# Where two feed-forwards split their matmul operands: VectorE in place of GpSimd, and activations split per column in the second

## The chip, the cores and the metric

The kernel runs on one core of a Trainium2 chip. The metric is the device time of the whole kernel in microseconds (us): the median of three runs. Its engines are TensorE (PE in the profile), which multiplies matrices and accumulates in PSUM; VectorE (DVE), ScalarE (ACT) and GpSimd (POOL), which work element by element in SBUF; and SyncE (SP), which here only starts transfers. Each engine works through its own queue in order. PEld is TensorE's loading of the stationary operand.

## What is computed

Two blocks of two layers each, on 256 rows of 1024 numbers (float32). The first block's layers have mixers (recurrent, dilated and latent attention) and a feed-forward, which is what changes; the second block's layers have attention and a table of 16384 experts per layer ("peer"), 128 of which are gathered for each row.

```python
# first block, layer l
h = rms_norm(x, attn_norm_g[l])
...
x = x + concatenate([ya, yb, yc]) @ w_out[l]
h = rms_norm(x, ffn_norm_g[l])
x = x + (silu(h @ ffn_w_gate[l]) * (h @ ffn_w_up[l])) @ ffn_w_down[l]
# second block: rows of its context and of x
s1, s2 = q1 @ sub_keys[0].T, q2 @ sub_keys[1].T     # two top-16, their 256 sums, top-16 of these
u = u_tab[expert]
act = gelu(einsum('nhkd,nd->nhk', u, hb))
out = einsum('nhk,nhkd->nd', softmax(top_s) * act, v_tab[expert])
```

The width of the feed-forward is 2816, that is 22 columns of 128.

## The kernel before, in words

**Splits.** Each float32 matmul is made of three: both operands are split into a high part (rounded, dtype F32R) and a low part (the rest), and hi*hi, hi*lo and lo*hi are accumulated (`mm3`, L183 to 191). `Net.split` (L172 to 181) makes the high part with a copy on ScalarE (L177) and the low part with a subtraction (L181) on VectorE, or on GpSimd where its argument `eng2` says so. Weights come as 512 KB tiles (128 x 1024); `Weights.load` splits them and goes through the letters of `low` in turn, "gv" being GpSimd, VectorE and so on.

**A feed-forward** (`First.ffn`, L509 to 547) has two loops of 22 steps. The gate/up loop loads two weight tiles (wgu) per column c, multiplies both with the normed and transposed x (hT) into one PSUM tile pgu, and makes the activation: a tanh on ScalarE (L523), then on VectorE a multiplication and addition in SBUF (L524), a product with the gate half (L525) and one with the up half (L526). The result of all columns, ffact, stands in SBUF in float32. The down loop loads one tile of ffn_w_down (wd) per step k, splits it, splits column k of ffact into a pair ffak (ffak_hi on ScalarE, ffak_lo on GpSimd), and adds 12 matmuls to four PSUM tiles pd. Behind the loop x_state (L547, four instructions on VectorE) adds pd to x.

**The two feed-forwards** are f0 (layer 0, L1791) and f1 (layer 1, L1820). f0 has two weight buffers of each kind and the letters "gv": of 44 wgu_lo 22 are on GpSimd, of 22 wd_lo 11. f1 has six buffers and "v": its 44 wgu_lo are on VectorE, but 5 of its 22 wd_lo (those that go through wd2) and all 22 ffak_lo are on GpSimd. Between them lies the mixer of layer 1, m1, whose norm makes nr_y on GpSimd, nr_t on VectorE, and transposes x into hT.

**What runs beside them.** The second block's context rows are routed and gathered at the same time. The routing (`route_block`, L1296 to 1392) is a chain of top-k steps on VectorE for each of two blocks of 128 rows; its ends are ef (L1386), the slots slot_e (L1389) and slot_eT (L1392, after a transpose stp on TensorE). The gather (`peer_gather`) asks for rows by an indirect DMA that GpSimd starts (ug, L1425), and makes a product of each with hm: on GpSimd (L1415, with ScalarE's sum L1416) for the first 60, on VectorE (a custom instruction, L1418) after these. After f1 come the final norm of the first block and the norm of the second (hxn, hxs, hxv, then nr_y and ns_y), and the weights wqkv of the first attention.

**The order** is not written out by hand: a scheduler with a model of the engines' time puts the instructions of all these parts into one order per engine, by rank and by when it thinks that they can start. A change of one part therefore moves rows of the others too.

## Time and profile before

| | |
|---|---|
| median of three runs | 3541.01 us (3537.23, 3541.01, 3547.21) |
| the profiled execution | 3555.65 us, its span 3553.9 us |
| mean granted TensorE clock | .935 of full |
| PE busy | 88% of the span |
| DVE busy | 74% |
| POOL busy | 54% |
| ACT busy | 40% |

The profile is one execution, 14.6 us longer than the median; times within it are microseconds from the start of its span. f0 takes the stretch from some 240 (gate/up) and 530 (down) to 627.5, m1 the one to 925, f1 the one from 925 (gate/up) and 1052.6 (down) to 1128.2. A share of busy time over the whole span says little about one of these stages, so the rows below are cut by stage. "PEclk" is the granted clock as a share of the full one.

### The profile page before, as it was taken

The page shows a single profiled execution, that of the slowest core. Times are in us where ns is not written, and L with a number is a line of the kernel's source. Part 1 is how long each engine was busy: PE and PEld are TensorE (multiplying, and loading weights), DVE is VectorE, ACT ScalarE, POOL GpSimd, SP SyncE. Part 2 cuts the span into 40 slices and gives each one's busy share as a digit, 9 for nine tenths or more (in the row PEclk, how much of TensorE's full clock was granted, in tenths as well). Part 3 has the DMA queues.
Part 4 walks back from the last instruction along what each step waited for, and adds up shares of the span by engine and source line. Part 5 has one row for each costly group of instructions (what it writes and reads, how often), then busy time and mean ns, then how long its engine had stood idle before and what let it go on. Part 6 is the DMA issues. An engine that isn't in the chain of part 4 may idle for free. (4 is left out here: it accounts for less than half of the span.)

```text
span 3553.9 us, 58408 instructions
## 1 busy us (share of the span) xinstructions
PE 3114.9 (88%) x22044; PEld 2575.2 (72%) x22044; DVE 2635.4 (74%) x5055; ACT 1426.0 (40%) x2195; POOL 1920.3 (54%) x1368
## 2 busy tenths in 40 slices
PE   8979997688896768879878899999888899999999
PEld 6758895566795558867557658756668899986887
DVE  5647789774897789999875784675677826789777
ACT  4234543443543454433323333323454343443454
POOL 2113228656667576667557657666211465544665
PEclk9999999899898879989989999999899999999999
DMA  6555554667897567778768779878423454544555
GB/s 205 174 165 162 161 161 155 205 218 238 301 331 248 174 224 243 240 276 312 247 232 306 274 265 322 306 280 322 143 68 118 154 178 155 167 155 137 183 191 172
DMA packets 260970, 761.46 MB, mean 214 GB/s; under 512 B 26064, under 2 KB 81424, under 8 KB 260688
## 3 DMA queue, kind: packets, MB, share of 16 engines
q1 hardware_dynamic: 127856, 410.50, 34.5%
q0 software_dynamic: 79456, 289.18, 23.7%
q10 hardware_dynamic: 53376, 58.05, 5.0%
q8 instruction: 173, 2.83, 0.3%
q14 instruction: 109, 0.89, 0.1%
HBM read 753.44 MB, written 4.19 MB: 213 GB/s over the span
## 5 line engine op out<-in xcount | busy, mean ns | idle before, releaser
L1582 PE MATMUL aT<-h_hi,u_lo 128*128 128x256 f32 x2048 | 595.6, 292 | 53.6 <-POOL u_lo L1567 26.7
L1580 PE MATMUL aT<-h_hi,u_hi 128*128 128x256 f32 x2048 | 595.0, 291 | 7.5 <-ACT u_hi L1564 6.8
L1581 PE MATMUL aT<-h_lo,u_hi 128*128 128x256 f32 x2048 | 588.4, 288 | 0.0
L1650 POOL TENSOR_TENSOR v_lo<-v_raw,v_hi 128x512 fp32r<-128x512 f32 x256 | 398.7, 1564 | 247.3 <-ACT v_hi L1649 223.4
L1567 POOL TENSOR_TENSOR u_lo<-u_raw,u_hi 128x512 fp32r<-128x512 f32 (+1 forms) x256 | 362.7, 1425 | 293.0 <-ACT u_hi L1564 284.8
L1425 POOL DMA_INDIRECT ug<-in_peer_u,slot_e x256 | 311.8, 1218 | 285.5 <-DVE act L1418 122.2
L1649 ACT ACTIVATE v_hi<-v_raw 128x1024 fp32r<-128x1024 f32 x256 | 270.8, 1059 | 477.6 <-issue 222.0
L1564 ACT ACTIVATE u_hi<-u_raw 128x1024 fp32r<-128x1024 f32 x256 | 269.5, 1058 | 477.4 <-PE aT L1581 216.2
L1582 PEld LDWEIGHTS aT<-h_hi,u_lo 128*128 128x128 f32 x2048 | 400.8, 196 | 68.3 <-DVE u_lo L1567 30.5
L1580 PEld LDWEIGHTS aT<-h_hi,u_hi 128*128 128x128 f32 x2048 | 402.6, 197 | 14.7 <-ACT u_hi L1564 9.0
L1581 PEld LDWEIGHTS aT<-h_lo,u_hi 128*128 128x128 f32 x2048 | 402.4, 196 | 4.2 <-issue 4.2
L1664 PE MATMUL acc<-v_hi,w_lo 128*128 128x512 f32 x1024 | 339.2, 413 | 60.2 <-DVE w_lo L181 59.5
L1567 DVE TENSOR_TENSOR u_lo<-u_raw,u_hi 128x512 fp32r<-128x512 f32 (+1 forms) x256 | 262.5, 1027 | 163.1 <-ACT u_hi L1564 138.7
L1449 POOL DMA_INDIRECT vg<-in_peer_v,slot_eT x256 | 262.6, 1026 | 142.1 <-PE pv L1454 59.7
L1664 PE MATMUL acc<-v_lo,w_hi 128*128 128x512 f32 x1024 | 331.4, 405 | 0.1
L1664 PE MATMUL acc<-v_hi,w_hi 128*128 128x512 f32 x1024 | 308.6, 411 | 5.2 <-ACT w_hi L177 5.2
L1415 POOL TENSOR_TENSOR ug<-ug,hm 128x1024 f32<-128x1024 f32 x106 | 263.4, 2489 | 65.9 <-DMA ug<-in_peer_u,slot_e 62.3
L1651 DVE TENSOR_TENSOR v_lo<-v_raw,v_hi 128x512 fp32r<-128x512 f32 x256 | 203.5, 795 | 116.0 <-ACT v_hi L1649 102.9
L1664 PEld LDWEIGHTS acc<-v_hi,w_lo 128*128 128x128 f32 x1024 | 192.4, 195 | 119.6 <-DVE w_lo L181 74.7
L181 DVE TENSOR_TENSOR w_lo<-d_A,w_hi 128x256 fp32r<-128x256 f32 x256 | 264.0, 1033 | 3.7 <-ACT w_hi L177 3.5
L1418 DVE CUSTOM_DVE_ANT_0 ug<-ug,hm 128x1024 f32<-128x1024 f32 x150 | 212.3, 1423 | 37.9 <-DMA ug<-in_peer_u,slot_e 35.4
L1664 PEld LDWEIGHTS acc<-v_lo,w_hi 128*128 128x128 f32 x1024 | 199.2, 196 | 45.9 <-issue 2.0
(659 smaller groups left out, 7539.3 us busy)
## 6 DMA issues: line engine op xcount, KB each, us to landing
u_raw<-in_u_columns SPq DMA_DIRECT2D x256, 512.0 KB
v_raw<-in_peer_v SPq DMA_DIRECT2D x256, 512.0 KB
adaw<-in_ada_w ACTq DMA_DIRECT2D x96, 512.0 KB
wgu<-in_ffn_w_gate SPq DMA_DIRECT2D x44, 512.0 KB
wgu<-in_ffn_w_up SPq DMA_DIRECT2D x44, 512.0 KB
wd<-in_ffn_w_down SPq DMA_DIRECT2D x44, 512.0 KB
wpq<-in_peer_w_q SPq DMA_DIRECT2D x32, 512.0 KB
wqkv<-in_w_qkv SPq DMA_DIRECT2D x24, 512.0 KB
```

The costliest lines, as they stand in the source:

```text
L181: e.tensor_tensor(lo, src, hi.bitcast(F32), op=ALU.subtract)
L1415: nc.gpsimd.tensor_tensor(u, u, hm, op=ALU.mult)
L1425: nc.gpsimd.indirect_dma_start(out=u, out_offset=None, in_=ut, in_offset=bass.IndirectOffsetOnAxis(ap=slots[b][0][:, j : j + 1], axis=0))
L1449: loads.append(nc.gpsimd.indirect_dma_start(out=four[q], out_offset=None, in_=vt, in_offset=bass.IndirectOffsetOnAxis(ap=slots[b][1][:, to ...
L1564: nc.scalar.activation(uh, u, AF.Copy)
L1567: e.tensor_tensor(ul[:, o:m], u[:, o:m], uh[:, o:m].bitcast(F32), op=ALU.subtract)
L1580: nc.tensor.matmul(o, uh[:, k], self.hh[:, k], start=k == 0, stop=False)
L1581: nc.tensor.matmul(o, uh[:, k], self.hl[:, k], start=False, stop=False)
L1582: nc.tensor.matmul(o, ul[:, k], self.hh[:, k], start=False, stop=k == KD - 1)
L1649: nc.scalar.activation(vh, v, AF.Copy)
L1650: nc.gpsimd.tensor_tensor(vl[:, 0:512], v[:, 0:512], vh[:, 0:512].bitcast(F32), op=ALU.subtract)
L1664: nc.tensor.matmul(self.acc[2 * b + hf], x[:, bs], y[:, hf * 512 : (hf + 1) * 512], start=s0, stop=s1)
```

## The change

In f0 the letter of the scope is "v", so all 44 wgu_lo and 22 wd_lo are on VectorE, and so are the 22 ffak_lo, since `split` is called without `eng2`. In f1 the 5 wd_lo of wd2 move to VectorE, and `early=True` replaces ffact by a pair of tiles, ffact_hi in zone "x" and ffact_lo in a new zone "y" (22528 bytes of each partition): the last product of a column goes back into ffth, and the column is split at once, high part on ScalarE and low part on VectorE. The down loop of f1 takes its operand from this pair and splits no activation. In all 82 subtractions go from GpSimd to VectorE. Line numbers of the new kernel are up to 11 higher from here on (x_state L558, slot_e L1400, the gather's products L1426 and L1429, its DMA L1436).

```diff
@@ -506,13 +506,17 @@
                 xs = x[:, b, hf * 512 : (hf + 1) * 512]
                 nc.vector.tensor_tensor(xs, pss[hf][b], xs, op=ALU.add)
 
-    def ffn(self, l, x, after=None, more=None):
+    def ffn(self, l, x, after=None, more=None, early=False):
+
 
         nc, n, a = self.nc, self.n, self.a
         hT, _ = self.norm_T(x, self.vcol("ffn_norm_g", l, 8), "hT2")
         if after:
             after()
-        act = self.zones["x"].tile([P, KF, S], F32, name="ffact")
+        if early:
+            act = self.zones["x"].tile([P, KF, S], F32R, name="ffact_hi"), self.zones["y"].tile([P, KF, S], F32R, name="ffact_lo")
+        else:
+            act = self.zones["x"].tile([P, KF, S], F32, name="ffact")
         for c in range(KF):
             ps = self.psum("pgu")
             for i, name in enumerate(("ffn_w_gate", "ffn_w_up")):
@@ -523,7 +527,11 @@
             nc.scalar.activation(th, ps[:, :S], AF.Tanh, scale=0.5)
             nc.vector.tensor_scalar(th, th, 0.5, 0.5, op0=ALU.mult, op1=ALU.add)
             nc.vector.tensor_tensor(th, ps[:, :S], th, op=ALU.mult)
-            nc.vector.tensor_tensor(act[:, c], ps[:, S:], th, op=ALU.mult)
+            if early:
+                nc.vector.tensor_tensor(th, ps[:, S:], th, op=ALU.mult)
+                n.split(th, *part(act, c))
+            else:
+                nc.vector.tensor_tensor(act[:, c], ps[:, S:], th, op=ALU.mult)
         wd = a["ffn_w_down"][l].rearrange("(k p) c -> p k c", p=P)
         pss = [self.psum(f"pd{i}") for i in range(4)]
         for k in range(KF):
@@ -535,9 +543,12 @@
                     two = self.zones["x"].pair([P, 2, D], "wd2")
                 w = part(two, k % 2)
                 raw = ws.plain(wd[:, k : k + 1], 1, D, "wd")
-                n.split(raw[:, 0], *w, eng2="gv"[k % 2])
-            ak = self.z.pair([P, S], "ffak")
-            n.split(act[:, k], *ak, eng2="g")
+                n.split(raw[:, 0], *w, eng2="v")
+            if early:
+                ak = part(act, k)
+            else:
+                ak = self.z.pair([P, S], "ffak")
+                n.split(act[:, k], *ak)
             for b in range(2):
                 for hf in range(2):
                     n.mm3(pss[2 * b + hf], part(ak, slice(b * P, (b + 1) * P)), part(w, slice(hf * 512, (hf + 1) * 512)), k == 0, k == KF - 1)
@@ -1705,7 +1716,6 @@
 GATHERS = 58
 MORE = 56
 UFIRST = EARLY + GATHERS + MORE - P
-LOW = "gv"
 POOL_DOTS = 3
 GATHER_CLASSES = ((32, 8), (512, 5), (1024, 2), (4096, 1))
 ATTN_CLASSES = (
@@ -1788,8 +1798,8 @@
                 for _ in itertools.islice(gather, SOON):
                     pass
                 slots.append(next(routed))
-            with f.scope("f0", FFN_ZONES, 2, {"w": 4}):
-                f.ffn(0, x, more=Weights(n, cw, 2, nc.sync, 2, LOW))
+            with f.scope("f0", FFN_ZONES, 2, {"w": 4}, "v"):
+                f.ffn(0, x, more=Weights(n, cw, 2, nc.sync, 2))
         tside.close()
         gside = cside.enter_context(ExitStack())
         gp[:] = [pool(gside, "g_g0", 2, side="right")]
@@ -1817,8 +1827,8 @@
                     pass
                 at[0] = tc.cur_priority
 
-        with f.scope("f1", FFN_ZONES, 6, {"w": 6}, "v", 4):
-            f.ffn(1, x, lambda: gather_on(GATHERS))
+        with f.scope("f1", dict(FFN_ZONES, y=((22528, 1),)), 6, {"w": 6}, "v", 4):
+            f.ffn(1, x, lambda: gather_on(GATHERS), early=True)
         fx.close()
         for l in range(L):
             last = l == L - 1
```

The scheduler's order changes with it. Three places:

VectorE at the end of f0, before: the second block's routing (csc to slot_e) and the four x_state.

```order
L1356 TENSOR_TENSOR csc_2305<-csc_2305 128x512 x2
L1356 TENSOR_TENSOR csc_2305<-csc_2305 128x256 x2
L1356 TENSOR_TENSOR i1o<-csc_2305 128x128
L1356 TENSOR_TENSOR i2o<-csc_2305 128x128
L1386 SCALAR_TENSOR_TENSOR ef<-i1o,i2o 128x128
L1389 CAST slot_e_3995<-ef 128x128
L547 TENSOR_TENSOR x_state<-pd_5684,x_state 128x512
L547 TENSOR_TENSOR x_state<-pd_5685,x_state 128x512
L547 TENSOR_TENSOR x_state<-pd_5686,x_state 128x512
L547 TENSOR_TENSOR x_state<-pd_5687,x_state 128x512
```

The last rows of the routing, down to the slots of the second block, stand ahead of x_state.

VectorE at the end of f0, in the changed kernel: csc_2305, v, i are the second block's routing at its first and second top-k step.

```order
L1324 MAX v_3997<-csc_2305 128x8 x3
L1403 CAST slot_eT_3777<-stp 128x128
L1324 MAX v_3997<-csc_2305 128x8 x9
L1323 MATCH_REPLACE csc_2305<-v_3997,csc_2305 128x128
L1325 MAX_INDEX i_3998<-v_3997,csc_2305 128x8 x3
L558 TENSOR_TENSOR x_state<-pd_5684,x_state 128x512
L558 TENSOR_TENSOR x_state<-pd_5685,x_state 128x512
L558 TENSOR_TENSOR x_state<-pd_5686,x_state 128x512
L558 TENSOR_TENSOR x_state<-pd_5687,x_state 128x512
L1325 MAX_INDEX i_3998<-v_3997,csc_2305 128x8 x9
L1324 MAX v_3997<-csc_2305 128x8
```

The rest of this routing, down to the slots, now stands behind x_state, between the rows of m1.

GpSimd at the start of m1, before: ug are products and requests of the gather, nr_y the norm of m1, w_lo one of its weights.

```order
L1415 TENSOR_TENSOR ug<-ug,hm_3945 128x1024 x2
L1425 DMA ug<-in_peer_u,slot_e_3776 128x1024 x2
L1415 TENSOR_TENSOR ug<-ug,hm_3945 128x1024
L212 TENSOR_TENSOR nr_y<-nv,mhalf 128x2
L1415 TENSOR_TENSOR ug<-ug,hm_3945 128x1024
L1425 DMA ug<-in_peer_u,slot_e_3776 128x1024
L181 TENSOR_TENSOR w_lo<-w,w_hi 128x896
```

Nearly all products of f0's time stand ahead of these rows.

GpSimd at the start of m1, in the changed kernel: these are also the first requests and products of the gather.

```order
L1420 DMA hm_3945<-d_crows 128x1024
L1436 DMA ug<-in_peer_u,slot_e_3776 128x1024 x2
L1426 TENSOR_TENSOR ug<-ug,hm_3945 128x1024 x2
L1436 DMA ug<-in_peer_u,slot_e_3776 128x1024 x2
L1426 TENSOR_TENSOR ug<-ug,hm_3945 128x1024
L181 TENSOR_TENSOR w_lo<-w,w_hi 128x896
L212 TENSOR_TENSOR nr_y<-nv,mhalf 128x2
L1426 TENSOR_TENSOR ug<-ug,hm_3945 128x1024
```

No split of f0 is left on GpSimd, and nr_y stands behind the first three products of all and a w_lo; in the kernel before seven products stood ahead of it, from f0 on.

VectorE at the end of f1, before: ISA ug,act are the gather's products (each followed by its read of the sum, act), hxs the sums of the norm.

```order
L547 TENSOR_TENSOR x_state<-pd_10249,x_state 128x512
L547 TENSOR_TENSOR x_state<-pd_10250,x_state 128x512
L547 TENSOR_TENSOR x_state<-pd_10251,x_state 128x512
L1418 ISA ug,act_3944<-ug,hm 128x1024
L1418 ISA act_3944 128x1
L1116 ISA hxj,hxs<-hxn,final_g 128x512
L1116 ISA hxs 128x1
L547 TENSOR_TENSOR x_state<-pd_10252,x_state 128x512
L1116 ISA hxj,hxs<-hxn,final_g 128x512
```

One product stands between the third x_state and the fourth.

VectorE at the end of f1, in the changed kernel: ident is a copy for the attention that follows.

```order
L558 TENSOR_TENSOR x_state<-pd_10297,x_state 128x512
L1429 ISA ug,act_3944<-ug,hm 128x1024
L1429 ISA act_3944 128x1
L558 TENSOR_TENSOR x_state<-pd_10298,x_state 128x512
L558 TENSOR_TENSOR x_state<-pd_10299,x_state 128x512
L1429 ISA ug,act_3944<-ug,hm 128x1024
L1429 ISA act_3944 128x1
L1038 CAST ident_10741<-c_all 128x128
L558 TENSOR_TENSOR x_state<-pd_10300,x_state 128x512
L1429 ISA ug,act_3944<-ug,hm 128x1024
L1429 ISA act_3944 128x1
L1127 ISA hxj,hxs<-hxn,final_g 128x512
```

From the first x_state to hxv five products stand in the changed kernel and two in the one before. In both six stand directly ahead of the first x_state.

## Rows read from the trace of the kernel before

**Rows 1.** The page: busy time of each engine, share of the span, instructions

```profile
PE 3114.9 (88%) x22044; PEld 2575.2 (72%) x22044; DVE 2635.4 (74%) x5055; ACT 1426.0 (40%) x2195; POOL 1920.3 (54%) x1368
```

**Rows 2.** Busy time of each engine by stretch, granted clock, DMA share

```profile
core 0: us, PE busy (x) PEld busy (x) DVE busy (x) ACT busy (x) POOL busy (x), PEclk, DMA share, GB/s
240.00:530.00 290.00, 274.71 (x1956) 256.00 (x1956) 215.89 (x442) 146.11 (x244) 86.64 (x66) 0.99 0.49 155
530.00:617.10 87.10, 70.17 (x265) 54.28 (x265) 86.83 (x288) 29.51 (x51) 72.42 (x44) 0.88 0.49 159
617.10:627.50 10.40, 0.47 (x1) 0.18 (x1) 10.33 (x18) 3.45 (x6) 6.95 (x4) 0.76 0.45 164
627.50:925.00 297.50, 236.30 (x1647) 173.01 (x1647) 187.69 (x321) 124.20 (x238) 189.93 (x111) 0.86 0.69 228
925.00:1052.60 127.60, 127.60 (x1058) 127.30 (x1056) 123.09 (x160) 63.79 (x94) 77.84 (x48) 1.00 0.90 321
1052.60:1128.20 75.60, 66.65 (x265) 52.59 (x264) 61.93 (x61) 27.87 (x43) 68.29 (x46) 0.91 0.72 246
1128.20:1152.00 23.80, 0.10 (x1) 0.00 (x0) 16.07 (x38) 6.66 (x12) 8.40 (x7) 0.56 0.88 318
```

**Rows 3.** Waits, 530 to 627.5: engine, line, for what; us, times, longest

```profile
PE pd L191 <- POOL ffak_lo L181: 9.1, 3, 6.4
...
PE stp L1391 <- DVE ef L1386: 7.8, 1, 7.8
...
PE pd L190 <- POOL wd_lo L181: 4.1, 2, 2.3
```

**Rows 4.** VectorE in order of time, 604 to 628: start, length, line, tiles

```profile
604.53 2.42 DVE L1341 TENSOR_SCALAR pm<-pm 128x128 int32<-128x128 int32 x1
...
625.00 2.48 DVE L547 TENSOR_TENSOR x_state<-pd,x_state 128x512 f32<-128x512 f32 x4
```

**Rows 5.** ffth in f0: min/median/max ns, first and last start

```profile
L524 DVE TENSOR_SCALAR ffth<-ffth x21: 280/2319/2549, 278.3 to 526.0; 128x256 f32<-128x256 f32 x21
L525 DVE TENSOR_TENSOR ffth<-pgu,ffth x21: 398/425/426, 280.7 to 526.6; 128x256 f32<-128x256 f32 x21
```

**Rows 6.** wgu_lo in f0, by engine

```profile
L181 DVE TENSOR_TENSOR wgu_lo<-wgu,wgu_hi x22: 1205/1225/1227, 256.0 to 520.6; 128x1024 fp32r<-128x1024 f32 x22
L181 POOL TENSOR_TENSOR wgu_lo<-wgu,wgu_hi x22: 2362/2399/3619, 259.5 to 522.6; 128x1024 fp32r<-128x1024 f32 x22
```

**Rows 7.** GpSimd in order of time, start of m1

```profile
628.66 2.35 POOL L1415 TENSOR_TENSOR ug<-ug,hm 128x1024 f32<-128x1024 f32 x1 [4.16 <-DMA ug<-in_peer_u,slot_e]
631.11 0.73 POOL L212 TENSOR_TENSOR nr_y<-nv,mhalf 128x2 f32<-128x2 f32 x1
```

**Rows 8.** TensorE in order of time, start of m1, idle before it in brackets

```profile
638.37 1.94 PE L415 MATMUL fps<-c_all,x_state 128*128 128x128 f32 x8 [8.87 <-DVE hT_lo L420]
```

**Rows 9.** VectorE by group, 925 to 1052.6: busy us, mean ns

```profile
L181 DVE TENSOR_TENSOR wgu_lo<-wgu,wgu_hi 128x1024 fp32r<-128x1024 f32 x40 | 69.2, 1735 | 3.6 <-ACT wgu_hi L177 3.6
L1418 DVE CUSTOM_DVE_ANT_0 ug<-ug,hm 128x1024 f32<-128x1024 f32 x24 | 31.3, 1308 | 0.0
```

**Rows 10.** Waits, 1052.6 to 1152: engine, line, for what; us, times, longest

```profile
PE pd L190 <- POOL wd_lo L181: 4.5, 2, 3.1
...
PE pd L189 <- ACT ffak_hi L177: 2.6, 1, 2.6
...
PE pd L191 <- POOL ffak_lo L181: 1.9, 2, 1.4
```

**Rows 11.** VectorE in order of time, end of f1 and the norm

```profile
1114.83 3.38 DVE L1418 CUSTOM_DVE_ANT_0 ug<-ug,hm 128x1024 f32<-128x1024 f32 x1
...
1130.89 1.22 DVE L1418 CUSTOM_DVE_ANT_0 ug<-ug,hm 128x1024 f32<-128x1024 f32 x1 [2.96 <-DMA ug<-in_peer_u,slot_e]
...
1132.04 1.88 DVE L547 TENSOR_TENSOR x_state<-pd,x_state 128x512 f32<-128x512 f32 x3
...
1140.50 1.23 DVE L1418 CUSTOM_DVE_ANT_0 ug<-ug,hm 128x1024 f32<-128x1024 f32 x1 [1.93 <-DMA ug<-in_peer_u,slot_e]
```

## What the change should do to the time

> **What bounds the kernel now.** I read the page's engine line first [rows 1]: TensorE is busy for 3114.9 of 3553.9 us and VectorE for 2635.4, so neither bounds the whole span, and the change is worth what its own stages can give back. So the second view is the table of stretches, cut where the stages of the two feed-forwards begin and end [rows 2]. The reader is to see four things in it. In the first feed-forward's gate/up stretch (240 to 530) TensorE has 274.7 of 290 us: it is the bound there, nearly. In the down projection after it (530 to 617.1) VectorE is busy for 86.83 of 87.1 us: VectorE is the bound, TensorE works 70.2 us at a mean granted clock of .88 (that is 61.7 us at the full 2.4 GHz), and TensorE then stands for 10 us more until 627.5. In the second feed-forward's gate/up stretch (925 to 1052.6) TensorE never stops. In its down projection (1052.6 to 1128.2) TensorE works 66.65 of 75.6 us at .91 (60.7 at full clock), and VectorE has slack.
>
> Then the waits of the first down projection [rows 3]: TensorE waits 9.1 us for GpSimd's ffak_lo, 4.1 for GpSimd's wd_lo, and at the end 7.8 for VectorE's ef, which belongs to the routing of the second block of rows. The list of VectorE's work in order of time shows why [rows 4]: the last matmul of pd ends at 617.1, but the four x_state additions start only at 625.00, because the routing stands ahead of them in VectorE's queue; its last part alone runs from 604.53 to 625.00.
>
> Last, what makes VectorE so full. The multiplication of ffth (L524, 128x256) takes 280 ns at best and 2319 at the median of 21 in the first feed-forward, while the next one on the same engine (L525), which reads PSUM, never leaves 398 to 426 [rows 5]. GpSimd's wgu_lo takes 2.36 to 2.40 us [rows 6]: the multiplication sits out one of these nearly every time.
>
> **The Trainium skill on this.** The page "SBUF — State Buffer", section "Who interferes with whom", says that VectorE and GpSimd share one pair of ports as an exclusive lock, taken by a VectorE instruction in a two-port mode or with two SBUF inputs, and that one with at most one SBUF input outside these modes doesn't contend. The rows on L524 and L525 agree. The same rule of the Trainium skill speaks against the change too: every split moved to VectorE has two SBUF inputs, and could be held up by what GpSimd still does there, the gather products.
>
> **Part 1, first feed-forward, gate/up.** 22 wgu_lo go from GpSimd to VectorE: 22 x 1.225 = +27 us [rows 6]. In return 19 of the 21 multiplications shown are above their best by about 2.04 us: -39 us. VectorE (215.9 of 290) has the room either way, so only what TensorE idles there (15.3 us) can change. I take -2, between 0 and -5.
>
> **Part 2, first feed-forward, down projection.** VectorE takes on 11 wd_lo at 1.225 (the same 128x1024 form as wgu_lo [rows 6]) and 22 ffak_lo, a form that VectorE doesn't run before; the nearest rows are those on 128x256, from .28 to .425 [rows 5]; I take .42, that of the row with two operands, as a subtraction has: 13.5 + 9.2 = +22.7 us. Two things leave. First, the order of the changed kernel has the routing of the second block cut off behind x_state: the last part alone ran 20.5 us [rows 4]. Undisturbed it would be some 17, but top-k steps ahead of it move too, so I keep 20.5. Second, the contention: when I add up every VectorE instruction of 530 to 617 at the fast tenth of its own form, 62 of the 86.8 us are left, so 25 us are waiting for GpSimd; in the new order GpSimd has no split left there and begins its gather products only near the end, so I leave 3 of it. VectorE is the bound up to x_state, so its time moves by the sum: 625 + 22.7 - 20.5 - 22 = 605, and 604 with a smaller backlog from part 1: **-21 us**. TensorE could not be done before 530 + 61.7 = 592, so VectorE still sets the end, and no more than -33 can come; I bound the term by -10 (12 us of waits stay) and -27.
>
> **Part 3, what was pushed into the next mixer (627.5 to 925).** The routing that now follows x_state adds, by the same form-by-form sum, 26 us to a stretch in which VectorE has 187.7 of 297.5 and TensorE 236.3 [rows 2]: busy shares of 63 and 79%, so neither engine is full, but chains of small steps run there, and each routing piece that is in front delays one. On GpSimd nr_y of the mixer's norm comes behind the first three gather products and a w_lo; in before the one product right ahead of it ran 2.35 us [rows 7]. Three are up to 7.1 us; VectorE's nr_t waits for nr_y with hT_lo queued behind, and TensorE for hT_lo (8.87 us already, [rows 8]). I take **+8**, a third of the moved work; the bounds are 0 (all in idle time) and +20.
>
> **Part 4, second feed-forward, gate/up.** The early split adds 22 ffact_lo to VectorE there at .42 (as in part 2): +9.2 us, onto 123.1 of 127.6. But five gather products fewer stand there in the new order, at 1.31 us [rows 9]: -6.5. So 125.8 of 127.6: VectorE just stays below TensorE. I take +1, between 0 and +8. The upper end is what contention can do: the 40 wgu_lo of this stretch already take 1.735 us in the mean against 1.225 undisturbed [rows 6, 9], 20 us in all, with no other split on GpSimd there, so its gather products must cause it. Were each new split held up like a wgu_lo, +.5 us, that is 11 us, and VectorE comes to 136.8, 9 above TensorE: the rival "lock". ScalarE's 22 copies to ffact_hi only move in time.
> The Trainium skill's rule on the shared pair, on the page named above, would have it so.
>
> **Part 5, second feed-forward, down projection.** The splits of the activation no longer stand between gate/up and the matmuls, and wd_lo takes 1.2 instead of 2.4 us. The waits of TensorE that go are 4.5 for wd_lo, 2.6 for ffak_hi and 1.9 for ffak_lo [rows 10]: 9.0 us, and with them some of the clock (66.65 us at .91 would be 60.7). VectorE's part is 18 wd_lo and about as many gather products, 45 us, so it isn't late. I take **-12** of 75.6, bounds -9 and -15; the transfer rate must rise from 246 GB/s to some 300, and 321 is seen one stretch earlier [rows 2].
>
> **Part 6, the norm after it (1128.2 to 1152).** In before TensorE stands for 23.8 us while VectorE makes x_state and the norm's sums, with gather products in between that wait for their transfer: x_state starts at 1132.04, behind a product that began at 1130.89, and the next but one begins at 1140.50, 4.8 us from one to the next [rows 11]. In the new order five products stand between the first x_state and hxv instead of two. Three more at 1.22 are 3.7 us if their rows have landed, and 14.4 at the spacing of 4.8. Two qkg loads and the sink load now stand on SP directly ahead of wqkv, since the new zone y lies over the memory of their targets until the last pd matmul; GpSimd's two copies of k and v stand ahead of the norm's nr_y for the same reason. The nearest row for such a late arrival is the product that waited 2.96 us for its rows [rows 11]; I take 2 for all of them. Together **+6**, bounds 0 and +13.
>
> **Sum.** -2 - 21 + 8 + 1 - 12 + 6 = -20 us. The profiled execution has 3555.65, so it would come to 3535.65; against the median of the runs shown, 3541.01 (14.6 lower), it is **3521**. All that follows 1152 I leave unchanged: the order there is nearly the same.
>
> **The rivals.** A measurement of this kernel can tell about 0.3%, 10.6 us, from no change.
> Larger: the routing falls wholly into idle time of the mixer, the products have landed. -2 - 25 + 0 + 0 - 15 + 3 = -39: 3502. For it: 110 us of VectorE's mixer stretch are idle [rows 2]. Against: it is one queue in order.
> Lock: gate/up of the second feed-forward becomes VectorE's, +9 instead of +1: 3529. For it: the 20 us that wgu_lo waits there already. Against: five products fewer.
> No change: the mixer pays for the moved routing in full (+26 instead of +8): -2: 3539. For it: the 8.87 us wait for hT_lo and a wait of 7.8 for ef were such chains.
> Slower: gather products that stand ahead of dense steps and whose rows haven't landed, at two places. At 4.8 us from one to the next, three ahead of nr_y cost 14 in the mixer beside the 8. And eleven stand between the last wd_lo and hxv: in before the products behind the last wd_lo begin at 1114.83, 13 us ahead of the stretch's end [rows 11]; with an end near 1115 they begin near 1102 and end at 1155, 13 us after the last that hxv waited for in before (1140.50 + 1.2). Parts 5 and 6 are then +13 together instead of -6. Sum -2 - 21 + 8 + 14 + 1 + 13 = +13: 3554. It makes the kernel slower from a spacing of about 4.6 us at all of them. Against: fewer products stand ahead of x_state in all than before, and GpSimd, which asks for the rows, has all its splits less to do.
> That the change doesn't do what it says can be excluded: the order shows no split of either feed-forward left on GpSimd.
>
> **How the numbers follow.** Chances: the forecast .42, larger .16, lock .10, no change .20, slower .12. The lock's 3529 lies at the edge of what counts as faster; .06 of it go there, .04 to the same. Faster .64, same .24, slower .12. The range leaves out the lower end of "larger" and the upper end of "slower": 3497 to 3552.
>
> **What would show it.** Right: in the new profile L524 is near 280 ns throughout the first feed-forward; x_state starts near 604; TensorE's waits for ffak_lo and wd_lo are gone; the down stretch of the second feed-forward takes about 63 us. Wrong: VectorE idle or waiting for gathered rows ahead of x_state or hxv; the mixer stretch longer by more than 20 us; TensorE waiting for wgu_lo in the second gate/up.

## The result, and the profile after

The changed kernel takes 3497.04 us (median of four, 3492.16 to 3500.18) against 3541.18 for the one before: 44 us less, a ratio of .9873 with an interval of .9854 to .9892. The forecast was 3521, with 3497 as the lower end of its range: the direction was right, the forecast gain of 20 us less than half of the measured one.

The absolute times of both kernels differ from one set of runs to the next (before has its median between 3540 and 3564 in the sets below), so kernels are compared within a set. In three later sets the changed kernel had .9923 (.9897 to .9949), .9902 (.9868 to .9936) and .9903 (.9882 to .9925) of before: 28 to 35 us less. So the forecast of 20 us is too small by 8 to 24. In one of these sets one execution of each kernel took some 4300 us at a granted clock of .65; medians below leave these two out.

The stretches of the first profile after, the columns as in [rows 2]:

```profile
240.00:530.00 290.00, 274.49 (x1958) 256.93 (x1956) 198.58 (x424) 145.73 (x241) 33.94 (x46) 0.98 0.50 159
530.00:594.30 64.30, 62.58 (x277) 50.62 (x277) 61.36 (x224) 26.28 (x45) 3.77 (x4) 1.00 0.57 189
594.30:600.50 6.20, 0.09 (x1) 0.00 (x0) 6.20 (x28) 3.86 (x6) 5.37 (x4) 0.71 0.62 203
600.50:893.90 293.40, 226.15 (x1620) 170.19 (x1620) 202.80 (x446) 122.50 (x239) 197.81 (x109) 0.88 0.71 230
893.90:1033.00 139.10, 132.08 (x1086) 128.32 (x1085) 132.28 (x174) 74.76 (x122) 81.60 (x49) 1.00 0.84 287
1033.00:1092.80 59.80, 59.80 (x267) 49.48 (x265) 52.88 (x76) 20.88 (x23) 28.80 (x22) 1.00 0.90 336
1092.80:1115.00 22.20, 0.36 (x3) 0.04 (x1) 17.50 (x40) 6.99 (x12) 7.69 (x7) 0.55 0.92 345
```

The lines answer to [rows 2]. The down projection of f0 has shrunk from 87.1 to 64.3 us and TensorE's clock in it is 1.00. GpSimd worked 72.42 us there and now 3.77. The mixer takes 293.4 us. The gate/up stretch of f1 is longer, 139.1, and VectorE is busy for 132.28 of it; the down projection of f1 is all TensorE's, 59.80 of 59.80. The norm takes 22.2. For f1 the cut in [rows 2] lies at another place: before's first pd matmul of f1 is at 1055.2, 2.6 us behind the end of its row. Counted to the first pd matmul in both, gate/up goes from 130.2 to 139.2 us and the down projection from 72.7 to 59.6; so the table below counts.

From these and two more profiles of before and three of the changed kernel (the runs e1, e16, e5, e12 and e15 below), this is when each stage is reached, in us from the start, as means. aT, acc and gated belong to the second block's expert layers: aT multiplies the columns of the table u, acc those of the table v, and gated takes acc out of PSUM at the end of a layer:

| reached | before (3) | changed (4) | step of the gain |
|---|---|---|---|
| first pd matmul of f0 | 534.5 | 528.8 | -6 |
| transposes of x_state, start of m1 | 631.7 | 600.1 | -26 |
| first gate/up matmul of f1 | 927.4 | 899.5 | +4 |
| first pd matmul of f1 | 1058.1 | 1038.3 | +8 |
| last pd matmul of f1 | 1130.9 | 1097.9 | -13 |
| transposes behind the norm | 1155.7 | 1119.7 | -3 |
| first aT matmul | 1399.9 | 1366.6 | +3 |
| first acc matmul | 1688.3 | 1666.5 | +12 |
| first gated product | 2526.2 | 2492.0 | -12 |
| last gated product | 3547.0 | 3517.2 | +4 |

Up to the norm the steps are steady: the profiles of one kernel agree within 3 us in each stretch of f1 and within 10 in m1. The -12 isn't: that stretch took 837.6, 839.8 and 836.2 us in before and 802.0, 833.4, 835.7 and 830.6 in the changed kernel. The 802.0 belongs to the set of the 44 us, in which before itself had 3541; its profile of 837.6 took 3555.65. Without this profile the step is -5, so the -12 isn't a gain that is shown.

### The profile page after: what moved, and what is told of

It reads as the page before. It is cut to its first block, busy times and chain, and to the rows that moved or that the text cites. A ratio compares the mean times of both kernels' runs of the same rounds, so it can differ in the third digit from the quotient of the medians.

```text
span 3490.4 us, 58380 instructions
## 1 busy us (share of the span) xinstructions
PE 3072.5 (88%) x22044; PEld 2561.7 (73%) x22044; DVE 2622.2 (75%) x5137; ACT 1424.7 (41%) x2195; POOL 1776.6 (51%) x1286
## 5 line engine op out<-in xcount | busy, mean ns | idle before, releaser
L1436 POOL DMA_INDIRECT ug<-in_peer_u,slot_e x256 | 313.8, 1226 | 313.7 <-DVE act L1429 152.1
L1578 DVE TENSOR_TENSOR u_lo<-u_raw,u_hi 128x512 fp32r<-128x512 f32 (+1 forms) x256 | 272.1, 1065 | 164.7 <-ACT u_hi L1575 164.3
L1460 POOL DMA_INDIRECT vg<-in_peer_v,slot_eT x256 | 264.1, 1032 | 145.5 <-PE pv L1465 68.8
L1426 POOL TENSOR_TENSOR ug<-ug,hm 128x1024 f32<-128x1024 f32 x106 | 267.5, 2527 | 81.2 <-DMA ug<-in_peer_u,slot_e 77.7
L1662 DVE TENSOR_TENSOR v_lo<-v_raw,v_hi 128x512 fp32r<-128x512 f32 x256 | 226.7, 886 | 104.7 <-ACT v_hi L1660 104.3
L181 DVE TENSOR_TENSOR w_lo<-d_A,w_hi 128x256 fp32r<-128x256 f32 x256 | 256.8, 1005 | 4.4 <-ACT w_hi L177 4.4
L1429 DVE CUSTOM_DVE_ANT_0 ug<-ug,hm 128x1024 f32<-128x1024 f32 x150 | 213.2, 1426 | 45.1 <-DMA ug<-in_peer_u,slot_e 45.0
```

What stands on the lines that cost most here:

```text
L181: e.tensor_tensor(lo, src, hi.bitcast(F32), op=ALU.subtract)
L1426: nc.gpsimd.tensor_tensor(u, u, hm, op=ALU.mult)
L1436: nc.gpsimd.indirect_dma_start(out=u, out_offset=None, in_=ut, in_offset=bass.IndirectOffsetOnAxis(ap=slots[b][0][:, j : j + 1], axis=0))
L1460: loads.append(nc.gpsimd.indirect_dma_start(out=four[q], out_offset=None, in_=vt, in_offset=bass.IndirectOffsetOnAxis(ap=slots[b][1][:, to ...
L1578: e.tensor_tensor(ul[:, o:m], u[:, o:m], uh[:, o:m].bitcast(F32), op=ALU.subtract)
```

## The experiments

### Both kernels again

> The kernel before, unchanged, for a second profile of it. The profile of before that the prediction used was 14.6 us above the median. Theory A (the 63 us between the two profiles are 37 us up to 1152 and 19 us of difference between executions in the rest): this profile, if nearer 3541, puts the first f1 matmul and the end of the norm within 3 us of before's 924.9 and 1152, and the stretch from 1683 to 2521 some 10 us shorter than 837.6. Theory B (the changed kernel really gains some 25 us after 1152): this profile still has about 837 us from 1683 to 2521.

Measured: .999 of before (.9972 to 1.0008). Norm's transposes at 1154.7, 839.8 us from the first acc matmul to the first gated product: theory B by its letter, but see e5.

> The kernel before once more, for a third profile of it: fps of the mixer at 627 to 632, the norm's transposes at 1152 to 1156, the stretch behind the norm 2389 to 2395 if it is steady in this kernel, elsewhere if it varies.

Measured: 1.0005 (.9986 to 1.0024), transposes at 636.2 and 1160.3, 4 us later than expected; stretch behind the norm 2389.7, as expected.

> The changed kernel, unchanged, for a second profile of it beside the kernels of these runs. In its first profile the dense stretch from the first acc matmul to the first gated addition took 802 us, against 837.6 and 839.8 in two profiles of before and 824 to 837 in the three mixed kernels. Theory A (that was one lucky execution): it takes 815 or more here and the whole gain is about 44 us. Theory B (the changed order really shortens it): 800 to 806 again.

Measured: .9923, 833.4 us: theory A on the stretch, so the changed order doesn't shorten it; but the whole gain is 28 us here, not 44. All four executions of the first set took 3492 to 3500 us, so the 802 is rather that set's than one execution's.

> The changed kernel a third time, as the measure for the other three of these runs. From the first profiles: the norm's transposes at 1115 to 1121, 31 to 38 us ahead of before; the whole 28 to 44 us faster than before, since the stretch behind the norm took 2369.5 and 2408.2 us in two executions of this same kernel. If instead the gain lies behind the norm too, that stretch is below 2380 again.

> The changed kernel once more. Theory A (it loses in the stretch behind the norm what it doesn't lose elsewhere, except on the first chip): that stretch 2400 to 2412 again, gain over before 26 to 36. Theory B (it varies from execution to execution): between 2369 and 2408.

Measured: .9902 and .9903; norm at 1121.5 and 1121.7. From there to the last gated product 2407.4 and 2404.9 us, and 2408.2 in e5, where the three profiles of before have 2389 to 2395. So in these sets the changed kernel gives back some 16 us behind the norm, of which 12 in one stretch (e17 below). Only in the first profile it didn't.

### Which feed-forward gives what

```diff
# e2: f0 as changed, f1 as before        # e3: f0 as before, f1 as changed
-    f.ffn(1, x, ..., early=True)        -    with f.scope("f0", ..., "v"):
+    f.ffn(1, x, ...)  # and its "g"     +    with f.scope("f0", ...):  # and its "g"
```

> Only the first feed-forward changed; the second as before. Theory A (parts add): x_state of f0 near 598, mixer of 294 to 298 us, f1 as before with 127.6 and 75.6 us: time 3541 less 28 to 31, so 3510 to 3513. Theory B (the order of the gather and routing, which moves with f0, is what costs the 11 us in f1's gate/up): f1's gate/up takes 135 or more here too, although it has no early split: time 3518 or more.

> Only the second feed-forward changed. Theory A (parts add, the early split makes VectorE the bound of f1's gate/up): gate/up near 139, down near 60, norm near 22: 7 us less than before, 3534. Theory B (the gather's order from f0 costs the 11 us): gate/up stays near 128, down 60: 3524 or less.

Measured: e2 .9909 (.9878 to .9939), 32 us less than before; e3 .9950 (.9930 to .9970), 16 us less. In e2 the transposes of m1 come at 599.4, the mixer takes 299.5, f1's gate/up 134.9 and its down loop 76.2. In e3 the three parts of f1 take 132.7, 59.7 and 19.0. So e2 gains what theory A says, but with 4 us lost in f1's gate/up without any early split, nearly as in theory B: 15 of the gather's products on GpSimd lie in that stretch in e2, 12 in before. e3's whole is near theory B's, its gate/up between the two. The parts add to 48 us, both together gave 28 to 44.

### The early split

```diff
-    f.ffn(1, x, lambda: gather_on(GATHERS), early=True)
+    f.ffn(1, x, lambda: gather_on(GATHERS))       # all splits on VectorE, no zone y
```

> The changed kernel, but f1 splits its activations in the down loop again, on VectorE (ffak_lo), with ffact in float32 and no zone y. Theory A (the early split costs 11 us in gate/up and gives some of it back in the down loop): gate/up near 128, down 64 to 68: 3491 to 3497, that is as fast as the changed kernel or a little faster. Theory B (the 11 us come from the gather's products, not from the early split): gate/up 136 or more and down 64 to 68: 3502 to 3506.

> The kernel without the early split (splits all on VectorE) again, now on the same chip as the changed kernel. Up to the norm it took as long as the changed kernel (1117.4 against 1115.0 and 1120.6). If the early split is worth what it does to these stretches, the two agree within 5 us; if it gives more, this one is slower by 8 or more.

Measured: .9874 (.9848 to .9899) and .9857 (.9824 to .9890); in the second set 3507.3 against 3530.0 for the changed kernel. Gate/up 135.0 and 134.3, nearer to theory B's 136, down 64.2 and 64.3, norm at 1117.4 and 1116.5. Up to the norm it is 3 to 5 us ahead: the early split moves 4 to 5 us from the down loop into gate/up and gains nothing. The other 20 us lie behind the norm, which neither theory had; what they come from isn't shown (e17 has a part).

### f0's down loop and gate/up apart

```diff
# e8: before, with f0's wd and ffak on VectorE, its wgu still "gv"
-                n.split(raw[:, 0], *w, eng2="gv"[k % 2])
+                n.split(raw[:, 0], *w, eng2="gv"[k % 2] if l else "v")
-            n.split(act[:, k], *ak, eng2="g")
+            n.split(act[:, k], *ak, eng2="g" if l else "v")
# e7 (in before) and e6 (in the changed kernel): two products
-            nc.vector.tensor_scalar(th, th, 0.5, 0.5, op0=ALU.mult, op1=ALU.add)
-            nc.vector.tensor_tensor(th, ps[:, :S], th, op=ALU.mult)
+            nc.vector.scalar_tensor_tensor(th, th, 1.0, ps[:, :S], op0=ALU.add, op1=ALU.mult)
-            nc.vector.tensor_tensor(act[:, c], ps[:, S:], th, op=ALU.mult)
+            nc.vector.scalar_tensor_tensor(act[:, c], th, 0.5, ps[:, S:], op0=ALU.mult, op1=ALU.mult)
```

> The kernel before, with only the wd_lo and ffak_lo of f0 on VectorE; f0's wgu_lo stay half on GpSimd, f1 as before. Theory A (the down loop's gain comes from its own splits): down loop to the transposes near 70 instead of 97, gate/up still 265: 22 to 27 us faster than before. Theory B (part of it is the backlog that VectorE brings from gate/up): 76 to 85, 12 to 20 us faster.

Measured: .9960 (.9945 to .9975). From the first pd matmul to the transposes 79.5 us, between 97 (before) and 70 to 73: theory B by its number. Two thirds of the 26 us come from the down loop's own splits and the order that goes with them. The stretch of the down loop in e8:

```profile
537.60:612.30 74.70, 66.47 (x265) 51.77 (x265) 72.34 (x234) 31.24 (x51) 22.88 (x13) 0.93 0.54 179
```

GpSimd works 22.88 us there, 3.77 in the changed kernel. VectorE's splits from the first pd matmul to the transposes, first in e8, then in the changed kernel, and GpSimd's products in e8 (busy us, mean ns):

```profile
L181 DVE TENSOR_TENSOR wd_lo<-wd,wd_hi 128x1024 fp32r<-128x1024 f32 x19 | 25.5, 1344 | 1.0 <-ACT wd_hi L177 1.0
L181 DVE TENSOR_TENSOR ffak_lo<-ffact,ffak_hi 128x256 fp32r<-128x256 f32 x22 | 14.1, 642 | 1.2 <-ACT ffak_hi L177 1.2
```

```profile
L181 DVE TENSOR_TENSOR wd_lo<-wd,wd_hi 128x1024 fp32r<-128x1024 f32 x18 | 21.8, 1218 | 2.9 <-ACT wd_hi L177 2.9
L181 DVE TENSOR_TENSOR ffak_lo<-ffact,ffak_hi 128x256 fp32r<-128x256 f32 x22 | 9.1, 417 | 0.0
```

```profile
L1417 POOL TENSOR_TENSOR ug<-ug,hm 128x1024 f32<-128x1024 f32 x6 | 15.6, 2614 | 9.0 <-DMA ug<-in_peer_u,slot_e 9.0
```

So the last third isn't the backlog of theory B: e8 leaves one more wd_lo to this stretch, some 1 us, as the forecast had it. Its same splits take 7 us longer (19 x .126 + 22 x .225), with six products of the gather on GpSimd beside them where the changed kernel has two. The rest of VectorE's work there is the same within 1 us (46.0 and 46.4, an estimate, form by form).

> The kernel before with the same two instructions instead of three, all splits where they were. If the multiplication L524 sitting out GpSimd's wgu_lo is what VectorE lost in f0's gate/up (38 us of VectorE), VectorE's busy time there falls by some 45 us, although GpSimd still makes half of the splits. Theory A (this loss also held up TensorE): f0's gate/up goes from 265 to 258, as with the change. Theory B (TensorE waits there for GpSimd's slow wgu_lo): it stays at 264 to 266. The down loop should keep its 97 us in both. Whole: 3541 less 5 to 12 in A, less 0 to 4 in B.

Measured: .9988 (.9973 to 1.0004), no change. VectorE is busy for 162.6 us of gate/up instead of 197.5, yet the stretch keeps its length (266.5 against 265): theory B. The down loop takes 102.4 where 97 was expected; why isn't known. So the 38 us that L524 sat out were real, and taking them away alone gained nothing.

> The changed kernel with the activation made by two instructions instead of three: (tanh + 1) * gate, then (* 0.5) * up, each with one operand in PSUM and one in SBUF. L524, which reads SBUF alone, is gone (44 x .28 us at best). Theory A (f1's gate/up is VectorE's, by its own work and by waiting for GpSimd): f1's gate/up falls from 139.2 to 128 to 133, f0's gate/up stays at 258 since TensorE sets it: 6 to 11 us faster than the changed kernel. Theory B (f1's gate/up waits for something else, ScalarE's or the gather's order): 137 to 140, no faster.

Measured: .9923 (.9908 to .9939), as e5 in the same set. f1's gate/up falls to 133.8, near theory A's 133, but the mixer takes 313.3 in the new order and the gain is gone. And a part of the wait moved to another instruction: ffact_lo, 416 ns undisturbed (e10) and 532 in the changed kernel, now takes 881 in the mean:

```profile
L181 DVE TENSOR_TENSOR ffact_lo<-ffth,ffact_hi 128x256 fp32r<-128x256 f32 x20 | 17.6, 881 | 0.1
```

### Does a GpSimd operation hold up VectorE?

```diff
# e9: behind the last product of a column     # e13: behind the split of the up weights
+    if c >= 4:                                +    if l == 0 and i == 1:
+        junk = self.z.tile([P, 4, S], ...)    +        junk = self.z.tile([P, KD, P], ...)
+        nc.gpsimd.tensor_tensor(junk,         +        nc.gpsimd.tensor_tensor(junk,
+            act[:, c-4:c], act[:, c-4:c])     +            w_hi, w_hi)
```

> The changed kernel with 18 useless subtractions on GpSimd in f0's gate/up loop: each takes 128x1024 of finished columns of ffact from themselves into a tile that nobody reads, the size of a wgu_lo. No VectorE instruction is added and nobody waits for the result. Theory A (a GpSimd tensor operation holds up the VectorE instruction L528, 128x256 from SBUF to SBUF, 283 to 291 ns in the changed kernel): some of the 22 instances grow to 1 to 2.5 us, each by what is left of the GpSimd operation; the two products with a PSUM operand stay at 405 to 426. Theory B (L524 was slow for another reason, the order of the splits): all stay below 300 ns.

Measured: L528 stayed at 282 to 290 ns in all 22, theory B by its letter. But these operations begin right behind a column's last product, and not one of them overlaps an L528 (the next is due 3 to 24 us later); the wgu_lo that do come then went up to 2801 ns (1214 to 1227 in the changed kernel). So the run could not tell the two apart for L528.

> The changed kernel with 22 useless subtractions on GpSimd in f0's gate/up, each as soon as the high part of the up weights is there, which is when GpSimd began its wgu_lo in before; the result is read by nobody. Theory A (a GpSimd tensor operation holds up L531, the former L524, for its whole length): the median of its 22 instances is 1.5 to 2.5 us as in before, the products with PSUM stay at .41 to .43. Theory B: its median stays below .4. Down loop and mixer as in the changed kernel, 70 and 293 to 303.

Measured, ffth and the useless tile in f0's gate/up (min/median/max ns):

```profile
L531 DVE TENSOR_SCALAR ffth<-ffth x22: 277/1982/1989, 287.5 to 537.5; 128x256 f32<-128x256 f32 x22
L532 DVE TENSOR_TENSOR ffth<-pgu,ffth x22: 406/424/425, 288.0 to 539.4; 128x256 f32<-128x256 f32 x22
...
L526 POOL TENSOR_TENSOR junk<-wgu_hi x22: 1885/2854/2960, 267.7 to 515.4; 128x1024 f32<-128x1024 f32 x22
```

The same instruction in the changed kernel:

```profile
L528 DVE TENSOR_SCALAR ffth<-ffth x22: 283/286/291, 286.0 to 531.2; 128x256 f32<-128x256 f32 x22
L529 DVE TENSOR_TENSOR ffth<-pgu,ffth x22: 412/424/425, 286.5 to 533.1; 128x256 f32<-128x256 f32 x22
```

Theory A. The multiplication goes from 286 to 1982 ns at the median, the product with a PSUM operand stays at 424, and the order on VectorE is the same but for one L531 that moved by a place. The GpSimd operation grows too, from 1885 at its shortest to 2854 at the median. One column shows both, in order of time (start, length, us); the last row is one without a VectorE operation beside its start:

```profile
385.68 1.23 DVE L181 TENSOR_TENSOR wgu_lo<-wgu,wgu_hi 128x1024 fp32r<-128x1024 f32 x1 [0.78 <-ACT wgu_hi L177]
385.72 2.94 POOL L526 TENSOR_TENSOR junk<-wgu_hi 128x1024 f32<-128x1024 f32 x1 [7.86 <-ACT wgu_hi L177]
386.82 1.99 DVE L531 TENSOR_SCALAR ffth<-ffth 128x256 f32<-128x256 f32 x1
...
402.48 1.90 POOL L526 TENSOR_TENSOR junk<-wgu_hi 128x1024 f32<-128x1024 f32 x1 [5.58 <-ACT wgu_hi L177]
```

GpSimd's operation begins .04 us after VectorE's wgu_lo and ends 1.75 us after the wgu_lo's end, so it takes 2.94 where the one alone takes 1.90. L531 begins as the wgu_lo ends, and is done .15 us after GpSimd's operation. This agrees with what the Trainium skill states in "SBUF — State Buffer", section "Who interferes with whom": a VectorE instruction in a two-port mode, which tensor_scalar can run in, contends with GpSimd for a shared pair of ports, and whoever issues first holds it for the whole instruction and blocks the other; a VectorE instruction with two SBUF inputs contends with a GpSimd one that reads SBUF; and one with at most one SBUF input, outside these modes, doesn't contend. No row here shows in which mode L531 runs.

And it costs TensorE time: f0's gate/up takes 264.1 us, against 256.2 to 257.7 without and 264.3 to 265.1 in before. This is one execution. From the first gate/up to the first pd matmul, in before, in the changed kernel and in e13:

```profile
265.70:530.70 265.00, 256.35 (x1875) 242.45 (x1875) 200.21 (x411) 128.08 (x208) 83.51 (x63) 1.00 0.51 162
272.50:530.20 257.70, 252.94 (x1863) 240.67 (x1862) 177.03 (x381) 126.58 (x205) 27.88 (x40) 1.00 0.52 164
272.50:536.60 264.10, 256.07 (x1864) 243.51 (x1862) 206.73 (x380) 126.41 (x203) 81.15 (x61) 0.99 0.49 160
```

### The products on GpSimd

```diff
-                if j < EARLY if b == 0 and j < EARLY + GATHERS else j % POOL_DOTS == 0:
+                if j < EARLY - 15 if b == 0 and j < EARLY + GATHERS else j % POOL_DOTS == 0:
```

> The changed kernel with the first 45 instead of 60 products of the gather on GpSimd, the other 15 on VectorE: these are the ones that GpSimd makes during f1's gate/up (15 x 2.50 us there). Theory A (waiting for GpSimd's products is what makes VectorE the bound of that stretch): wgu_lo falls from 1867 ns in the mean to below 1350, VectorE works 15 x 1.22 more on products and some 25 us less in waiting, gate/up falls from 139 to 128 to 132: 7 to 11 us faster than the changed kernel up to the norm. Theory B (VectorE's own work is the bound): 138 to 145, not faster.

Measured: .9853 (.9817 to .9890), 3505.15 us against 3530.0 for the changed kernel in the same set. f1's gate/up takes 130.9 us instead of 138.9, theory A; in the norm after it 4 us go again (26.2 instead of 22.0). VectorE's groups in gate/up, first in the changed kernel of this set, then here (busy us, mean ns):

```profile
L181 DVE TENSOR_TENSOR wgu_lo<-wgu,wgu_hi 128x1024 fp32r<-128x1024 f32 x42 | 76.8, 1828 | 11.2 <-ACT wgu_hi L177 11.2
L1429 DVE CUSTOM_DVE_ANT_0 ug<-ug,hm 128x1024 f32<-128x1024 f32 x17 | 23.5, 1382 | 0.0
```

```profile
L181 DVE TENSOR_TENSOR wgu_lo<-wgu,wgu_hi 128x1024 fp32r<-128x1024 f32 x41 | 50.3, 1226 | 11.1 <-ACT wgu_hi L177 10.1 <-PE pgu L191 1.0
L1429 DVE CUSTOM_DVE_ANT_0 ug<-ug,hm 128x1024 f32<-128x1024 f32 x34 | 41.2, 1211 | 0.0
```

VectorE does 17 products more, 18 us, and its splits take 26 us less. TensorE's 130.9 us are nearly all work (129.99, from the table of this stretch), and VectorE works 118.23 us where e12 has 130.68. Taking the GpSimd work onto VectorE made VectorE less busy.

An estimate from the lengths in the traces puts a price on it. I add up what every VectorE instruction of f1's gate/up takes above an undisturbed one of its form, and count GpSimd's products there: 26 us with 12 products in before, 32 with 15 in e2 and e4, 33 with 14 in e12, 35 with 15 in the first profile of the changed kernel, 1 with none in e10. That is 2.1 to 2.5 us for each product in all profiles of this stretch, whichever instruction is hit: in e2 the wgu_lo have a lower mean than in before (1658 against 1735), but L528, with 810, bears more.

```diff
# e14: e4 and e10 together
```

> Both of the kernels that were 25 us faster than the changed kernel on one chip, together: f1's activations split in the down loop, and 45 instead of 60 products on GpSimd. Theory A (the products on GpSimd cost f1's gate/up 8 us, the early split nothing that the down loop doesn't give back): gate/up 128 to 131, down 64 to 66, norm 19 to 24: up to the norm within 4 us of fewer products alone (1113), the whole within 8 us of it. Theory B (the two remove different losses): 10 us or more faster than either.

Measured: .9869 (.9848 to .9890), 3517.31 against 3534.27 for the changed kernel (e15). The norm's transposes come at 1112.4 and the whole is no faster than either: theory A, although gate/up (133.0) and down (60.5) both miss their ranges, in opposite directions. That the two remove the same loss isn't shown, though: from the first gate/up matmul of f1 to the norm they add, with 213.4 us against 216.7 in e10, 217.1 in e11 and 219.4 to 221.1 in the changed kernel.

### What is given back behind the norm

```diff
+                if b == 0 and 118 <= j < 123:
+                    nc.vector.memset(act[:, j : j + 1], 0.0)
+                    yield
+                    continue
                 u = row(j, "ug")
```

> The changed kernel without five of the gather's 256 products of u and their requests (numbers 118 to 122 of the first block of rows, all of which run behind the norm); their five results are set to zero, so a part of the context's expert layer is left out. Up to the norm the order is the same, so 1115 to 1122 there. Theory A (products pushed behind the norm lengthen the first sweep over u, where VectorE is busy for 96% of the time): 286 to 293 us from the first aT to the first acc matmul instead of 297 to 305. Theory B (the sweep is longer for another reason): 296 or more.

Measured: .9823 (.9797 to .9849), where before has 3539.7. The sweep from the first aT to the first acc matmul takes 289.6 us: theory A. The stretch in before (e16), in the changed kernel (e12) and here:

```profile
1405.60:1695.10 289.50, 240.88 (x2215) 218.61 (x2215) 271.71 (x658) 109.63 (x139) 197.08 (x165) 0.91 0.77 268
```

```profile
1368.00:1666.40 298.40, 239.98 (x2215) 217.71 (x2215) 279.78 (x678) 110.18 (x141) 204.69 (x170) 0.92 0.77 267
```

```profile
1365.10:1654.70 289.60, 240.05 (x2214) 218.75 (x2214) 268.35 (x644) 108.92 (x139) 204.75 (x167) 0.91 0.78 273
```

VectorE is the fullest engine there, 271.71 of 289.50 us in before and 279.78 of 298.40 in the changed kernel; with five products less 268.35 of 289.60. Most other kernels agree: 109 products done before the norm's end go with 288 to 294 us (before, e1, e16, e3), 106 to 108 with 288 to 293 (e2, e4, e6, e10, e11, e14), 111 with 292 (e8), 104 with 297 to 305 (all profiles of the changed kernel, e9, e13). One doesn't: e7 has 109 and takes 296.2. So leaving out five products, with their requests and transfers, brings back some 10 of the sweep's 12 us. How the products that the changed order pushed behind the norm lengthen it is not shown: hardly by lying in it, for VectorE makes 30 of them there in before, 31 in the changed kernel and 31 in e17. Nor is it shown that they explain the rest of what e4, e10 and e11 gain over the changed kernel: the order behind the sweep changes with them.

## Why the prediction was right in direction and wrong in size

The forecast was about the parts up to the norm. There the gain is 36 us in the mean of the profiles, not 20. The terms that were mis-sized most are the start of x_state in part 6 (+6 became -3), the contention in part 2 (-21 became -26), the idle time in part 1 (-2 became -6) and, the other way, the room on VectorE in part 4 (+1 became +8). Behind the norm the forecast put nothing, and in three of four profiles 16 us are given back there. So where the whole came nearest to the forecast, at 28 us, two errors that partly cancel had a part in it.

**Part 1** (-2 forecast, -6 measured; -8 from the first gate/up matmul on). That L524 would fall to 280 ns throughout held (283 to 291, above). The step that failed is that only TensorE's idle time could change and that contention there was VectorE's matter. By the rows under e13 TensorE idles for 4.8 us there instead of 8.7, and works 252.94 instead of 256.35: 12 of the matmuls recorded in that stretch in before lie elsewhere now. e13 puts 6 to 8 us back by GpSimd's operation alone. TensorE then waits 5.0 us for VectorE's wgu_lo, where the profiles of the changed kernel have 1.5 to 2.5, and its own work takes 3 us more at a granted clock of .99 instead of 1.00; by which instruction the hold-up reaches TensorE wasn't tested apart. e7 shows that removing L524's loss alone doesn't help TensorE.

**Part 2** (-21, -26). The mechanism was right: x_state starts at 598.0 instead of 604, VectorE's queue has the routing behind it, and the contention is gone (wd_lo at 1218 ns in the mean, ffak_lo at 417, where I took 1225 and 420). The step that was mis-sized is the contention: I took 22 us of waiting for GpSimd away and left 3, of which nothing was to be seen. From the first pd matmul to the transposes VectorE's busy time fell by 29 us (96.46 to 67.36). The routing that left is 20 of them, as forecast; the splits add 19 and not 22.7, since 4 of the 22 wd_lo run ahead of this stretch now; so some 28 us of waiting went (an estimate, added up form by form). TensorE works 62.58 of 64.30 us there now, at full clock.

**Part 3** (+8, +4). Three products and a w_lo ahead of nr_y: GpSimd in order of time at the start of m1 in the changed kernel:

```profile
602.33 2.34 POOL L1426 TENSOR_TENSOR ug<-ug,hm 128x1024 f32<-128x1024 f32 x1 [2.18 <-DMA ug<-in_peer_u,slot_e]
604.63 2.92 POOL L181 TENSOR_TENSOR w_lo<-w,w_hi 128x896 fp32r<-128x896 f32 x1
607.65 0.72 POOL L212 TENSOR_TENSOR nr_y<-nv,mhalf 128x2 f32<-128x2 f32 x1
```

nr_y begins 9.6 us after x_state, in before 6.1 ([rows 4, 7]). TensorE's wait for hT_lo, [rows 8], is 10.28 instead of 8.87:

```profile
600.52 1.97 PE L415 MATMUL fps<-c_all,x_state 128*128 128x128 f32 x8 [6.13 <-DVE x_state L558]
612.77 1.94 PE L415 MATMUL fps<-c_all,x_state 128*128 128x128 f32 x8 [10.28 <-DVE hT_lo L420]
```

That is the part of the 8 which came true. VectorE is busy for 202.80 us of the mixer, 15 more than in before, and the stretch grows by 4 in the mean of the profiles (295.7 to 299.4). So most of the routing lies in idle time, but not all: in every profile of the changed kernel TensorE waits 2 to 3 us for the routing's ef there and once 6.2 for a w_lo on VectorE, which it doesn't in before, while other waits shrank. Which of them make up the 4 isn't shown.

**Part 4** (+1, +8). The step that failed is that five fewer products on VectorE would make the room. VectorE's groups in f1's gate/up in the first profile of the changed kernel, against [rows 9]:

```profile
L181 DVE TENSOR_TENSOR wgu_lo<-wgu,wgu_hi 128x1024 fp32r<-128x1024 f32 x42 | 78.4, 1867 | 8.6 <-ACT wgu_hi L177 8.6
L1429 DVE CUSTOM_DVE_ANT_0 ug<-ug,hm 128x1024 f32<-128x1024 f32 x17 | 23.5, 1382 | 0.0
L181 DVE TENSOR_TENSOR ffact_lo<-ffth,ffact_hi 128x256 fp32r<-128x256 f32 x19 | 10.1, 532 | 0.0
```

TensorE's waits in that stretch (us, times, longest):

```profile
PE pgu L191 <- DVE wgu_lo L181: 4.2, 6, 1.2
...
PE pgu L190 <- DVE hT_lo L420: 2.8, 3, 1.6
```

The mean of wgu_lo rose from 1735 to 1867, and the new ffact_lo take 532 instead of 416, with 15 products on GpSimd there instead of 12; without any (e10) both are undisturbed. TensorE's wait for wgu_lo is what the prediction named as a sign of being wrong. That is the rival "lock" with about its price (+9). I had seen that the later gather would move GpSimd's products, and counted only those on VectorE. Two smaller changes cancel: 28 matmuls that ran in the mixer in before (ada, adat) lie in this stretch now, some 2.4 us by e10's 129.99 against 127.60, and before's wait of 2.6 for ffak_hi ahead of the first pd matmul is gone.

**Part 5** (-12, -13). Right in each of its steps: the three waits of [rows 10] are gone, TensorE works 59.80 us without a gap.

**Part 6** (+6, -3). The step that failed is that x_state would start as late as in before, behind a product that waits for its rows: 4.1 to 5.3 us after the start of the last pd matmul there, but in the changed kernel .9 to 1.4 us ahead of it (its first part needs only the first of the sums). That is some 6 us less, a wait that the forecast kept without saying so. VectorE at the end of f1, against [rows 11]:

```profile
1090.34 1.22 DVE L1429 CUSTOM_DVE_ANT_0 ug<-ug,hm 128x1024 f32<-128x1024 f32 x1 [1.37 <-DMA ug<-in_peer_u,slot_e]
...
1091.49 0.69 DVE L558 TENSOR_TENSOR x_state<-pd,x_state 128x512 f32<-128x512 f32 x1
...
1092.57 1.23 DVE L1429 CUSTOM_DVE_ANT_0 ug<-ug,hm 128x1024 f32<-128x1024 f32 x1 [0.40 <-DMA ug<-in_peer_u,slot_e]
...
1094.92 1.80 DVE L1429 CUSTOM_DVE_ANT_0 ug<-ug,hm 128x1024 f32<-128x1024 f32 x1
...
1097.79 1.21 DVE L1429 CUSTOM_DVE_ANT_0 ug<-ug,hm 128x1024 f32<-128x1024 f32 x1
...
1099.55 1.21 DVE L1429 CUSTOM_DVE_ANT_0 ug<-ug,hm 128x1024 f32<-128x1024 f32 x1
...
1104.34 1.22 DVE L1429 CUSTOM_DVE_ANT_0 ug<-ug,hm 128x1024 f32<-128x1024 f32 x1 [2.96 <-DMA ug<-in_peer_u,slot_e]
```

The first row stands ahead of x_state. Of the five behind it the first waits .40 us and the last 2.96, the others not at all. So the three more products cost about what the prediction took for landed rows, 3.7: from the first x_state to hxv it is 14.2 to 16.4 us, and 12.0 to 12.2 in before. Of the 2 us for late transfers nothing is to be seen: from hxv to the transposes it is 7.2 to 8.7 us against 8.0 to 8.1. And the spacing of 4.8 us in before is not the gather's pace as such; what set it there wasn't tested. Between the last wd_lo and x_state five products stand, not six.

**Behind the norm** (0, some +16 in three of four profiles). "All that follows 1152 I leave unchanged" is wrong: the sweep, where VectorE is busy for 94% and more of the time in these profiles of before, got 12 us longer, and five products less give 10 of them back (e17). The other 4 us or so, and what e4, e10 and e11 gain there, are open. Why the first set gained 44 us and the others 28 to 35 stays open too; in its profile it lies in the stretch between the first acc matmul and the first gated product (802.0 against 831 to 836, and 798.2 in e17). In these two executions the granted clock is .96 in that stretch, against .94 in the other three profiles of the changed kernel, and both come from the sets in which before has 3540 to 3541 instead of 3559 to 3564. No profile of before was taken in either, so it isn't known whether before has the short stretch there as well.

## What to carry to other kernels

Where an operation of one engine holds up another's, it costs what it holds up as well as its own time: here a product of some 2.4 us on GpSimd cost VectorE more than the 1.2 us that the same product takes on VectorE itself. Moving 82 subtractions onto the busier engine made it less busy (2635.4 us of the span before, 2622.2 and 2591.7 in two profiles after), and moving 15 products more did so again (2576.6 in e10). When work moves off an engine, ask which of its other work slides into the gap and beside whom, and count what is pushed past the last stage looked at. And a victim taken away (e6) leaves the cause: another instruction waits.

## What the runs showed of the hardware that was not expected

A GpSimd tensor operation of 1.885 us stretches a VectorE multiplication of .286 us to 1.98 (e13), and is itself stretched to 2.85 by VectorE's splits. In both directions the engine that waits shows as busy. The custom product on VectorE (128x1024, 1206 ns at its shortest in the changed kernel) took up to 4075 ns (948.48 to 952.56) beside a product on GpSimd (949.06 to 951.47).
